# Layer 1 of a two-layer trunk: split input weights stored to DRAM in the first half of the tokens and loaded in the second

## The chip, the cores and the metric

One core of one Trainium2 chip runs the whole program. The time is the device time of one execution in microseconds; the median of three runs is compared.

## The reference, cut to what matters

The trunk has two layers over 2048 tokens of 1024 features, each `x = x + rms_norm(layer(rms_norm(x)))`. Layer 0 is attention beside a gated MLP. Layer 1, where the change lies, is a convolution module:

```python
def conv_layer(h, w_in, dw_w, dw_b, ln_g, ln_b, w_out):
    a, gl, z = jnp.split(h @ w_in, 3, axis=-1)
    y = a * jax.nn.sigmoid(gl)
    y = lax.conv_general_dilated(y, dw_w[:, None, :], window_strides=(1,),
                                 padding=((CONV_KERNEL - 1, 0),),
                                 dimension_numbers=('NWC', 'WIO', 'NWC'),
                                 feature_group_count=CONV_WIDTH) + dw_b
    y = jax.nn.silu(layer_norm(y, ln_g, ln_b))
    return (y * jax.nn.silu(z)) @ w_out
```

`w_in` is 1024 x 3072 and the depthwise convolution has 31 taps per channel. All data is float32.

## The kernel before

**Split products.** Float32 products are made of three matmuls on two rounded parts: an operand is cast to a high part (`hi`) and the remainder is kept as a low part (`lo`), and `hi*hi + hi*lo + lo*hi` is accumulated (`dense_T`, L152 to L165). The method `split` (L119 to L125) makes the parts: a cast on ACT (L122), then a subtraction (L125), on POOL for the weights of this layer.

**Layer 1, input.** `layer1_in` (L957) is run for tokens 0 to 1023 and again for tokens 1024 to 2047 (its argument `half`). Each half goes through the same 12 blocks of 256 weight columns, in slightly different orders (`GATED`, L45): eight of kind "g" (128 columns of `a` and 128 of the gate) and four of kind "z" (256 columns of `z`). So there are 24 blocks, numbered 0 to 23 here and `i` in the code. A block is four groups of 24 matmuls of 128x512; each group is a step of the generator, and a call of `beat` stands behind it. The inner function `load` (L963) fetches a block's weights into `wraw` (one buffer, 1 MB; L972, DMAs at L976) and splits them into `whiA`/`wloA` or `whiB`/`wloB`, in turn (L978 to L981). `weights` (L985) calls it one block ahead: the load of block i+1 is written at the start of block i, when the matmuls of block i-1, which used the same pair of tiles, have been issued.

**The convolution.** Each "g" block gives one `y` tile (128 channels, 1024 tokens), which joins a queue; its 31 taps are shared out between DVE and POOL. DVE does a tap in one instruction (`acc`, L1134). POOL needs a product by ACT (`prod`, L1100) and adds it (`cacc`, L1101). A finished channel block goes to `yc_d` in DRAM (L1143).

**The planner.** Who does which tap is settled while the program is written: `self.clock` has a booked time for DVE ("v") and POOL ("p"), `beat` (L1158) moves the planner's time by 5.12 us and gives out taps until both clocks have caught up, first to POOL and then to DVE. A tap books 1.2 us on DVE (L1136) or 2.4 us on POOL (L1102). Other work of these engines books time as well, so that fewer taps fall to them: a weight split books 4.5 us on POOL (L982).

**The tail.** `tail` (L1270) writes the steps in order: first half, the second half's normalised input (`load_hs`), second half with the first three chunks of `gated_norm` between its steps, then eight chunks of 256 tokens of output projection (`out2`), with the layer norm of the chunk two further on (`gated_norm`, L1175) between them. The norm of chunk 4 and later needs every channel of the convolution of the second half (`drain`, L1148 and L1186). The output weights are split by DVE (L1324).

**Order.** Each engine runs its queue in order. The build sorts the instructions into the queues by its own estimate of when each can start, with the written order as a guide, so neighbours in a queue are not always neighbours in the code. All DMAs of this layer are issued by SP, in the order of its queue: one that waits holds those behind it.

Of the kernel before, what the change touches and what calls it, by code (L numbers as in the profile page):

```python
# [10 lines left out]
F32 = mybir.dt.float32  # L11
F32R = mybir.dt.float32r
# [7 lines left out]
P = 128  # L20
S = 2048
D = 1024
KT = D // P
# [58 lines left out]
class Trunk:  # L82
# [151 lines left out]
    def setup(self):  # L234
        nc = self.nc
        self.odd = self.pool(self.ctx, "odd")
        edge = [self.pool(self.ctx, f"edge{side}", side=side) for side in (None, "right")]
        edge[0].tile([P, LEFT // 4], F32, name="left", tag="left")
        edge[1].tile([P, RIGHT // 4], F32, name="right", tag="right")
        c = self.c = self.pool(self.ctx, "const")  # L240
        dr = self.dr = self.pool(self.ctx, "spill", 1, DRAM)
        self.q_d = dr.tile([2, 512, S], F32, name="q_d", tag="q_d")
        self.ksw_d = dr.tile([2, 256, S], F32, name="ksw_d", tag="ksw_d")
        self.vsw_d = dr.tile([S, 4, P], F32, name="vsw_d", tag="vsw_d")
        self.kvc_d = dr.tile([256, S], F32, name="kvc_d", tag="kvc_d")
        self.a_d = dr.tile([D, S], F32, name="a_d", tag="a_d")
        self.bz_d = dr.tile([D, S], F32, name="bz_d", tag="bz_d")
        self.x1_d = dr.tile([S, D], F32, name="x1_d", tag="x1_d")
        self.yc_d = dr.tile([D, S], F32, name="yc_d", tag="yc_d")
        self.z_d = dr.tile([D, S], F32, name="z_d", tag="z_d")  # L250
        self.taps = self.tile(c, [P, KT, TAPS], F32, "taps")
        self.cb = self.tile(c, [P, KT], F32, "cb")
        self.ident = self.tile(c, [P, P], F32, "ident")
        make_identity(nc, self.ident)
        self.gpre = self.tile(c, [P, 2, KT], F32, "gpre")
# [701 lines left out]
    def layer1_in(self, inner, half, hs):  # L957

        nc, a, pool, conv = self.nc, self.a, self.lp, self.cp
        W = a["odd_w_in"][0]  # L960
        t0 = half * HALF

        def load():  # L963
            i = len(self.ws)
            if i == 24:
                return
            kind, k = self.plan[i]
            if kind == "g":
                pieces = [W[:, n * D + P * k:n * D + P * k + P] for n in range(2)]
            else:  # L970
                pieces = [W[:, 2 * D + 256 * k:2 * D + 256 * k + 256]]
            raw = self.tile(pool, [P, KT, 256], F32, "wraw")  # L972
            o = 0
            for p in pieces:
                w = p.shape[1]
                nc.sync.dma_start(raw[:, :, o:o + w], p.rearrange("(k p) n -> p k n", p=P))  # L976
                o += w
            where, tag = ((pool, "A"), (inner, "B"))[i % 2]  # L978
            hi = self.tile(where, [P, KT, 256], F32R, "whi" + tag)
            lo = self.tile(where, [P, KT, 256], F32R, "wlo" + tag)  # L980
            self.split(hi, lo, raw, nc.scalar, nc.gpsimd)  # L981
            self.busy("p", 4.5)  # L982
            self.ws.append((hi, lo))

        def weights():  # L985
            i = self.nw
            self.nw += 1
            while len(self.ws) < min(24, i + 2):
                load()
            return self.ws[i]  # L990

        def gated(k):
            w = weights()
            y = self.tile(conv, [P, HALF + 32], F32, "y", 6)
            if half:
                nc.scalar.copy(y[:, 0:32], self.hist[:, k])
            else:
                nc.gpsimd.memset(y[:, 0:32], 0.0)
            th = self.tile(pool, [P, 2, 512], F32, "b4", 5)
            for c in range(2):  # L1000
                o, = self.dense_T(w, P, hs[c:c + 1])
                nc.scalar.activation(th[:, c], o, AF.Tanh, scale=0.5)
                self.beat()
                yield
            for c in range(2):
                o, = self.dense_T(w, 0, hs[c:c + 1])
                nc.vector.scalar_tensor_tensor(y[:, 32 + 512 * c:544 + 512 * c], th[:, c], 1.0, o,  # L1007
                                               ALU.add, ALU.mult)
                self.busy("v", 0.6)
                if c == 0:  # L1010
                    self.beat()
                    yield
            if not half:
                nc.scalar.copy(self.hist[:, k], y[:, HALF:])
            self.queue.append(dict(k=k, half=half, y=y, tap=0, end=TAPS, acc=None, sum=None, bias=self.cb[:, k:k + 1]))
            self.beat()
            yield

        def zgate(k):
            w = weights()  # L1020
            st = [self.tile(pool, [P, 2, 512], F32, "b4", 5) for _ in range(2)]
            for c in range(2):
                for j in range(2):
                    o, = self.dense_T(w, P * j, hs[c:c + 1])
                    nc.scalar.activation(st[j][:, c], o, AF.Silu)  # L1025
                    self.beat()
                    yield
            for j in range(2):
                r = 256 * k + P * j
                nc.sync.dma_start(self.z_d[r:r + P, t0:t0 + HALF], st[j].rearrange("p c t -> p (c t)"))  # L1030

        for kind, k in self.plan[12 * half:12 * half + 12]:
            yield from (gated if kind == "g" else zgate)(k)
# [377 lines left out]
```

## Time and profile before

| what | value |
|---|---|
| runs | 2277.89, 2279.05 and 2279.7 us; median 2279.05 us |
| the profiled execution's own time | 2275.86 us |
| its span, first to last instruction | 2274.1 us |
| mean granted TensorE clock | 0.992 |
| busy, share of the span | PE 97%, DVE 68%, POOL 62%, ACT 55% |
| the first half's blocks begin at | 1520 us |
| the second half's block 14 begins at | 1839.7 us |
| output projection of layer 1 begins at | 2068.1 us |

Times within the execution are microseconds from the first instruction. A line such as L1134 is a line of the kernel. In a row of a group, "x304 | 378.9, 1281 | 4.0" means 304 instructions, 378.9 us busy in all, 1281 ns each in the mean, and 4.0 us in which the engine stood idle just before them. In a timeline row the first number is the start, the second the duration, and a bracket at the end gives the idle time before it and what ended it. PEclk is the granted TensorE clock as a share of full speed; the two levels are 2.4 GHz (1.00) and 1.2 GHz (0.50).

### The profile page before, as it was taken

Reading aid. Unit: us, or ns where it says so; the run is one execution under the profiler, and the core shown is the slowest. Engines: PE = TensorE matmul, PEld = TensorE weight load, DVE = VectorE, ACT = ScalarE, POOL = GpSimd, SP = SyncE. Lnnn points to the kernel's source line nnn. Section 1 sums busy time; section 2 is a strip of 40 time slices with the busy share of each in tenths; the row PEclk is TensorE's granted clock in tenths of the full one; section 3 lists DMA queues with packets and bytes.
Section 4 is the critical chain, followed back from the end, with each engine's and each line's share of the span. In section 5 each row is a group of like instructions: output and inputs, shape, how many; then the busy total and the mean of one; then the engine's idle time right before and its main releaser. Section 6 shows DMA issues by size and latency. Waiting matters only on the chain.

```text
span 2274.1 us, 34588 instructions
## 1 busy us (share of the span) xinstructions
PE 2202.5 (97%) x12414; PEld 1907.0 (84%) x12414; DVE 1547.0 (68%) x3272; ACT 1258.6 (55%) x2345; POOL 1400.6 (62%) x1351
## 2 busy tenths in 40 slices
PE   8999999999989999999999989999999989998998
PEld 7898889988878999898998978888888778886877
DVE  3441324365248998888889844527998899999772
ACT  5231232253258888878898854425555575556463
POOL 5232222243237778667789644548999579999683
PEclk9999999999999999999999999999999999999999
DMA  6252231442281111100113154651222432224641
GB/s 161 94 190 88 79 107 53 145 138 86 89 235 53 32 41 29 29 22 25 29 54 110 45 169 151 215 187 47 84 75 83 139 111 65 74 93 145 226 167 65
DMA packets 244860, 229.19 MB, mean 101 GB/s; under 512 B 33841, under 2 KB 206897, under 8 KB 244432
## 3 DMA queue, kind: packets, MB, share of 16 engines
q1 hardware_dynamic: 244688, 226.98, 31.5%
q8 instruction: 98, 1.61, 0.3%
q14 instruction: 74, 0.61, 0.1%
HBM read 157.73 MB, written 69.21 MB: 100 GB/s over the span
## 4 chain that ended last, share of the span: by engine, by line
PE 64%; DVE 15%; POOL 10%; issue 5%; ACT 3%; DMA 2%; SPq 1%; DVEq 0%; POOLq 0%; ACTq 0%
POOL cacc L1101 7%; PE T L708 7%; PE A L161 7%; PE A L162 7%; PE A L163 7%; DVE acc L1134 6%; PE O L731 4%; PE A L576 4%; PE O L730 4%; PE A L577 4%; PE A L844 4%; PE A L843 4%; PE A L842 4%; PE A L173 2%; PE A L175 2%
## 5 line engine op out<-in xcount | busy, mean ns | idle before, releaser
L1134 DVE SCALAR_TENSOR_TENSOR acc<-y,const_taps,acc 128x1024 f32<-128x1024 f32 x304 | 378.9, 1281 | 4.0
L1101 POOL TENSOR_TENSOR cacc<-cacc,prod 128x1024 f32<-128x1024 f32 x145 | 371.7, 2569 | 14.5 <-ACT prod L1100 7.2
L125 POOL TENSOR_TENSOR wlo<-wraw,whi 128x2048 fp32r<-128x2048 f32 (+1 forms) x26 | 120.8, 4647 | 314.8 <-ACT whi L122 279.5
L125 DVE TENSOR_TENSOR ptl<-T,pth 128x512 fp32r<-128x512 f32 (+1 forms) x414 | 263.8, 659 | 20.8 <-ACT pth L122 17.9
L122 ACT CAST pth<-T 128x512 fp32r<-128x512 f32 (+1 forms) x414 | 221.6, 579 | 50.4 <-PE T L708 40.3
L1100 ACT ACTIVATE prod<-y,const_taps 128x1024 f32<-128x1024 f32 x145 | 165.2, 1149 | 139.1 <-POOL cacc L1101 138.9
L161 PE MATMUL A<-hhi,whi 128*128 128x512 f32 x608 | 237.8, 391 | 0.0
L163 PE MATMUL A<-hhi,wlo 128*128 128x512 f32 x608 | 236.8, 389 | 0.0
L162 PE MATMUL A<-hlo,whi 128*128 128x512 f32 x608 | 236.8, 389 | 0.0
L685 POOL TENSOR_SCALAR Ps<-Ps,attn_ssm,gates 128x256 f32<-128x256 f32 (+15 forms) x128 | 161.1, 1259 | 110.9 <-DVE attn_ssm L682 77.9
L730 PE MATMUL O<-pth,V 128*128 128x256 f32 x824 | 220.7, 292 | 0.0
L731 PE MATMUL O<-ptl,V 128*128 128x256 f32 x824 | 219.5, 293 | 1.0 <-POOL ptl L717 0.4
L576 PE MATMUL A<-K,q 128*128 128x320 f32 (+4 forms) x544 | 206.7, 384 | 9.0 <-DVE attn_smx L580 4.4
L577 PE MATMUL A<-K,q 128*128 128x320 f32 (+4 forms) x544 | 183.7, 343 | 0.0
L680 ACT ACTIVATE Ps<-Ps,attn_nm 128x256 f32<-128x256 f32 (+15 forms) x128 | 155.8, 1217 | 31.3 <-DVE attn_nm L678 29.2
L580 DVE CUSTOM_DVE_ANT_1 Ps<-A,attn_bm 128x512 f32<-128x512 f32 (+3 forms) x264 | 154.8, 611 | 22.9 <-PE A L577 11.4
L708 PE MATMUL T<-ident,Ps 128*128 128x128 f32 x1088 | 164.3, 273 | 2.2 <-DVE ptl L125 1.8
L731 PEld LDWEIGHTS O<-ptl,V 128*128 128x128 f32 x824 | 155.6, 189 | 8.5 <-DVE ptl L125 4.2
L730 PEld LDWEIGHTS O<-pth,V 128*128 128x128 f32 x824 | 155.7, 189 | 2.5
L162 PE MATMUL A<-h,whiA 128*128 128x512 f32 x384 | 151.1, 394 | 0.0
L161 PE MATMUL A<-h,whiA 128*128 128x512 f32 x384 | 150.3, 393 | 0.7 <-DVE y L1007 0.7
L161 PE MATMUL A<-h,whiB 128*128 128x512 f32 x384 | 149.7, 390 | 1.2 <-ACT b L1025 1.2
(388 smaller groups left out, 6197.1 us busy)
## 6 DMA issues: line engine op xcount, KB each, us to landing
wraw<-in_even_w_in_dram SPq DMA_DIRECT2D x24, 1024.0 KB, 6.0
q<-q_d SPq DMA_DIRECT2D x128, 128.0 KB, 2.8
wraw<-in_odd_w_in_dram SPq DMA_DIRECT2D x32, 512.0 KB, 4.6
x<-x_d SPq DMA_DIRECT2D x21, 512.0 KB, 3.3
a_d<-osum SPq DMA_DIRECT2D x128, 64.0 KB, 2.1
x<-in_x_dram SPq DMA_DIRECT2D x16, 512.0 KB, 5.6
x_d<-x SPq DMA_DIRECT2D x16, 512.0 KB, 2.6
wraw<-in_odd_w_in_dram SPq DMA_DIRECT2D x8, 1024.0 KB, 4.9
```

Of the source, the lines that this page charges most:

```text
L122: self.nc.scalar.copy(hi, src)
L125: lo_eng.tensor_tensor(lo, src, hi.bitcast(F32), ALU.subtract)
L161: nc.tensor.matmul(o, whi[:, k, wk], hhi[:, k], start=(k == 0), stop=False)
L162: nc.tensor.matmul(o, whi[:, k, wk], hlo[:, k], start=False, stop=False)
L163: nc.tensor.matmul(o, wlo[:, k, wk], hhi[:, k], start=False, stop=(k == KT - 1))
L576: nc.tensor.matmul(out, q[:, 0, r, :], K[:, g, ks], start=True, stop=False)
L577: nc.tensor.matmul(out, q[:, 1, r, :], K[:, g, ks], start=False, stop=True)
L708: nc.tensor.transpose(pt[:, c:c + P], ps[r], self.ident)
L730: nc.tensor.matmul(O, v, hi[:, c], start=(i + j == 0), stop=False)
L731: nc.tensor.matmul(O, v, lo[:, c], start=False, stop=(i + j == len(items) - 1))
L1101: nc.gpsimd.tensor_tensor(c["sum"], c["sum"], t, ALU.add)
L1134: v.scalar_tensor_tensor(acc, win, w, old, ALU.mult, ALU.add)
```

## The change

Blocks 0 to 11 split their weights as before, and each then writes the two parts to a DRAM tile of its kind and number, `w_d`, with two DMAs of 1 MB. Blocks 12 to 23 issue two DMAs of 1 MB that load the ready parts straight into the `whi` and `wlo` tiles; they load no `wraw`, make no cast and no subtraction, and book nothing on POOL's clock.

```diff
+        self.w_d = dr.tile([12, 2, P, KT * 256], F32, name="w_d", tag="w_d")
...
             kind, k = self.plan[i]
+            where, tag = ((pool, "A"), (inner, "B"))[i % 2]
+            hi = self.tile(where, [P, KT, 256], F32R, "whi" + tag)
+            lo = self.tile(where, [P, KT, 256], F32R, "wlo" + tag)
+            flat = lambda t: t.rearrange("p k n -> p (k n)").bitcast(F32)
+            kept = self.w_d[k + 8 * (kind == "z")]
+            if i >= 12:
+                for t, d in zip((hi, lo), kept):
+                    nc.sync.dma_start(flat(t), d)
+                self.ws.append((hi, lo))
+                return
             if kind == "g":
...
-            where, tag = ((pool, "A"), (inner, "B"))[i % 2]
-            hi = self.tile(where, [P, KT, 256], F32R, "whi" + tag)
-            lo = self.tile(where, [P, KT, 256], F32R, "wlo" + tag)
             self.split(hi, lo, raw, nc.scalar, nc.gpsimd)
+            for t, d in zip((hi, lo), kept):
+                nc.sync.dma_start(d, flat(t))
             self.busy("p", 4.5)
             self.ws.append((hi, lo))
```

## Rows read from the trace of the kernel before

**Rows 1.** The profile's page: busy time and share of each engine.

```profile
PE 2202.5 (97%) x12414; PEld 1907.0 (84%) x12414; DVE 1547.0 (68%) x3272; ACT 1258.6 (55%) x2345; POOL 1400.6 (62%) x1351
```

**Rows 2.** Busy time by stretch; after the engines granted clock, DMA share, GB/s.

```profile
1500.00:1760.00 260.00, 260.00 (x1148) 215.06 (x1147) 211.11 (x172) 136.33 (x149) 227.59 (x103) 1.00 0.26 87
1760.00:1880.00 120.00, 109.14 (x494) 88.14 (x493) 110.17 (x90) 71.12 (x89) 83.33 (x29) 0.97 0.36 119
1880.00:2060.00 180.00, 180.00 (x796) 149.06 (x795) 178.98 (x143) 102.58 (x105) 175.28 (x64) 1.00 0.23 80
2060.00:2110.00 50.00, 41.40 (x164) 32.91 (x163) 46.74 (x40) 28.61 (x35) 49.02 (x18) 0.90 0.52 178
2110.00:2200.00 90.00, 84.50 (x364) 68.87 (x363) 76.89 (x70) 48.35 (x86) 64.72 (x25) 0.98 0.55 196
```

**Rows 3.** Timeline of PE, 2060 to 2110 us: all three matmuls that waited.

```profile
2073.48 0.50 PE L843 MATMUL A<-h,h 128*128 128x512 f32 x1 [2.26 <-DVE h L125]
...
2085.22 0.50 PE L843 MATMUL A<-wloB,h 128*128 128x512 f32 x1 [1.43 <-DVE wloB L125]
...
2100.86 0.77 PE L842 MATMUL A<-whiA,h 128*128 128x512 f32 x1 [4.92 <-DVE yn L874]
```

**Rows 4.** Timelines of DVE and POOL in the same stretch.

```profile
2073.35 9.62 DVE L1134 SCALAR_TENSOR_TENSOR acc<-y,const_taps,acc 128x1024 f32<-128x1024 f32 x8
...
2083.42 15.04 POOL L1101 TENSOR_TENSOR cacc<-cacc,prod 128x1024 f32<-128x1024 f32 x4 [0.43 <-ACT prod L1100]
```

**Rows 5.** Groups by line and shape, 1500 to 2110 us.

```profile
L1134 DVE SCALAR_TENSOR_TENSOR acc<-y,const_taps,acc 128x1024 f32<-128x1024 f32 x304 | 378.9, 1281 | 4.0
...
L1101 POOL TENSOR_TENSOR cacc<-cacc,prod 128x1024 f32<-128x1024 f32 x145 | 371.7, 2569 | 14.5 <-ACT prod L1100 7.2
L125 POOL TENSOR_TENSOR wloA<-wraw,whiA 128x2048 fp32r<-128x2048 f32 x12 | 56.5, 4706 | 20.0 <-ACT whiA L122 19.9
L125 POOL TENSOR_TENSOR wloB<-wraw,whiB 128x2048 fp32r<-128x2048 f32 x12 | 56.0, 4664 | 4.6 <-ACT whiB L122 2.8 <-PE T L212 1.8
...
L1100 ACT ACTIVATE prod<-y,const_taps 128x1024 f32<-128x1024 f32 x145 | 165.2, 1149 | 139.1 <-POOL cacc L1101 138.9
L122 ACT CAST whiB<-wraw 128x2048 fp32r<-128x2048 f32 x13 | 24.8, 1907 | 8.1 <-PE A L162 7.6 <-DMA wraw<-in_odd_w_out_dram 0.5
```

**Rows 6.** Timelines of PE and POOL: blocks 22 and 23 begin; block 23's low part.

```profile
2024.59 0.39 PE L161 MATMUL A<-h,whiA 128*128 128x512 f32 x1
...
2046.35 0.39 PE L161 MATMUL A<-h,whiB 128*128 128x512 f32 x1
...
2033.39 4.61 POOL L125 TENSOR_TENSOR wloB<-wraw,whiB 128x2048 fp32r<-128x2048 f32 x1
```

**Rows 7.** Waits of SP's queue, 1500 to 2274 us: total, times, longest.

```profile
SPq L976 <- POOL wloB L125: 113.0, 10, 18.8
...
SPq L976 <- POOL wloA L125: 111.0, 12, 17.9
```

**Rows 8.** DMA issues, 1500 to 2110 us; then GB/s in 40 slices of 1760 to 1880 us.

```profile
wraw<-in_odd_w_in_dram SPq DMA_DIRECT2D x8, 1024.0 KB, 4.9
z_d<-b SPq DMA_DIRECT2D x16, 512.0 KB, 2.6
...
GB/s 0 175 8 175 0 124 374 26 175 0 8 167 125 366 210 241 338 124 0 29 288 340 372 159 215 0 0 0 0 175 175 5 0 115 235 3 0 0 0 0
```

**Rows 9.** Timeline of SP: a store of the convolution behind block 22's start.

```profile
2035.65 0.32 SPq L1143 DMA_DIRECT2D yc_d<-cout  x1
```

**Rows 10.** Timelines of DVE, POOL and PE, 1824 to 1865 us; last, L1214's group.

```profile
1824.77 5.58 DVE L1214 TENSOR_TENSOR y<-x,Y 128x1024 f32<-128x1024 f32 x1
...
1824.64 4.62 POOL L125 TENSOR_TENSOR wloA<-wraw,whiA 128x2048 fp32r<-128x2048 f32 x1 [4.54 <-ACT whiA L122]
...
1864.87 0.77 PE L1207 MATMUL T<-y,mean 128*128 128x256 f32 x1 [4.32 <-DVE y L1203]
...
L1214 DVE TENSOR_TENSOR y<-x,x 128x1024 f32<-128x1024 f32 x2 | 2.4, 1222 | 3.1 <-DMA x<-yc_d 3.1
```

## The prediction, made before the changed kernel was run

> **What bounds the kernel now.** I read the page's busy times first: PE is busy for 97% of the span, all others far less [rows 1]. A share of the whole span hides stages, so the table by stretch comes next [rows 2]. From 1500 to 1760 us and from 1880 to 2060 us PE is busy without a break at a granted clock of 1.00: there the projection's matmuls are the time, and nothing that is taken from another engine can shorten them. What can be won lies where PE stands idle: 120 - 109.14 = 10.86 us between the halves, 50 - 41.40 = 8.60 us at the start of the output projection (2060 to 2110), 5.50 us behind it. In the second stretch the clock is also 0.90 of full, that is at 1.2 GHz for part of it, after each of three idle times; 0.10 x 50 = 5.0 us are lost by that.
>
> The second thing to see in that table is what DVE and POOL do: from 1880 to 2060 they are busy for 178.98 and 175.28 of 180 us. Both run the taps of the convolution at their limit beside a PE that is at its own, and they fall behind it. The timeline of PE shows the bill: the three waits from 2060 to 2110 are ended by DVE, twice by a split of output weights and once by the work on an output tile [rows 3]. The timelines of DVE and POOL show what stands in the queue around those: runs of taps, eight in a row on DVE at 2073 and four on POOL from 2083 [rows 4]. So the unfinished convolution sets the loss in this stretch, and PE's own work sets the rest.
>
> **What the change removes.** In the second half 12 casts on ACT and 12 subtractions on POOL: 12 x 1.91 = 22.9 us of ACT and 12 x 4.69 us (the mean of 4.706 and 4.664) = 56.2 us of POOL [rows 5]. Alone that would buy nothing where PE is the limit. But the planner's bookings go too: 12 x 4.5 = 54 us of POOL's clock are free, and the planner fills them with taps. If n taps pass from DVE to POOL and both then end T sooner, 2.4 n = 54 - T and 1.2 n = T, so n = 15 and T = 18. Going through the bookings beat by beat, with whole taps and the sums that join the two engines' parts, I get 14 more sums on POOL and 13 fewer instructions on DVE, and the last tap given out three beats (15.4 us) sooner. In measured durations [rows 5]: DVE is 13 x 1.281 = 16.7 us ahead at the end of the convolution; POOL 56.2 - 14 x 2.569 = 20.2 us; ACT 22.9 - 14 x 1.149 = 6.8 us.
>
> **What that is worth.** Each wait from 2060 to 2110 is at most 4.92 us [rows 3], less than either lead, and the work that delayed it is what got shorter. So I count all 8.60 us of idle time and, with them, the 5.0 us of low clock: 13.6 us. The waits after 2110 (5.50 us) I leave as they are: there DVE works on the norms, with 76.89 of 90 us busy and no convolution [rows 2]. The 10.86 us between the halves I leave too; bounds of 0 and 14.5 us (10.86 and 0.03 x 120 = 3.6 of clock) go into the range.
>
> **What it adds in the first half.** 24 stores of 1 MB. No row has a store of 1 MB. One of 0.5 MB landed after 2.6 us, and neighbouring transfers reached 374 GB/s in a slice [rows 8]. Two stores (2.10 MB) thus take between 5.6 us (2.10 / 0.374) and 10.4 us (4 x 2.6). I take 6.8: 2.6 for the first half megabyte and 1.57 / 0.374 = 4.2 for the rest, as DMAs that are issued together overlapped in the rows. On SP the stores wait for the end of the subtraction. The next `wraw` load waits for the same event already (113.0 and 111.0 us of waits in all) [rows 7], so the stores' wait holds nothing that was free to go. But the load now lands behind the stores. That makes a ring: stores 6.8, load 4.9 [rows 8], cast 1.9, one tap ahead on POOL 2.6, subtraction 4.7, in all 20.9 us. A block takes 2046.35 - 2024.59 = 21.76 us, and the low part was ready at 2038.00, 8.35 us before its use [rows 6]. The ring is shorter than a block, so I cost it at nothing; matmuls of the block before cover it. With the upper end of 10.4 us it is 24.5 us, longer than a block, and the cover would be used up. That is the slower rival below.
>
> **What it adds in the second half.** Two loads of 1 MB a block, in place of one. They can start only when the block before last has released its tiles, since the prefetch into `wraw` one block earlier is gone. One load landed after 4.9 us [rows 8]; two take between 5.6 us and 9.8 us, and I take 4.9 + 1.05 / 0.374 = 7.7. Of a block's 21.76 us some 14 are spare, against 8.35 before. The new wait on PE is SP's; behind it in the queue stand stores of `z_d` and `yc_d` and loads for the norms. These hold the weights as well where they come first. The store of a finished channel block left at 2035.65, 11.06 us after block 22 had begun [rows 9], because DVE was late with it. Weights queued behind it would land at 2035.97 + 7.7 = 2043.7, still 2.7 us before 2046.35; with 9.8 us, 0.6 us before. With DVE 16.7 us further on such a store leaves sooner. I cost this at nothing, with little to spare. Instruction counts, the DRAM tile and the moved lines that allocate tiles cost nothing in a stretch that PE fills.
>
> **The sum** is made on the profiled execution: 2275.86 - 13.6 = 2262.3 us (its span of 2274.1 lies 1.8 below its own time). That execution is 3.2 us below the median of 2279.05, so for the median the same saving gives 2279.05 - 13.6 = 2265.4 us.
>
> **Rival 1: more is won, between the halves too** (2251 to 2259). At 1824.77 DVE began a sum (L1214) that took 5.58 us; the same instruction took 1.22 us elsewhere. POOL's subtraction ran from 1824.64 for 4.62 us, and the chain behind the sum made PE wait 4.32 us at 1864.87 [rows 10]. The subtraction goes. If half of the 14.5 us goes with it, the time is 2265.4 - 7.2 = 2258.2; if all, 2250.9. Against it: POOL fills the place with norm sums and taps of 2.57 us [rows 5], and DVE meets those instead.
>
> The Trainium skill (SBUF — State Buffer, section "Who interferes with whom") says that a DVE instruction with two SBUF inputs and a GpSimd instruction that reads SBUF exclude each other for a whole instruction. The row above agrees: 5.58 us is about the 4.62 us of the subtraction and 1.22 us of work less the 0.13 us between their starts, 5.71 us. By that rule shorter POOL instructions shorten the longest wait, but 14 more of them leave many chances for a short one.
>
> **Rival 2: the saving meets the next wait** (about 2275). The longest of the three waits, 4.92 us, ended with the work on an output tile, which needs results of PE and ACT besides DVE's turn. If only the two weight splits come sooner, 2.26 + 1.43 = 3.7 us are saved: 2275.4. For it: DVE and PE take turns in the tail, so a lead on one does not last. Against it: taps lie between the pieces of that work.
>
> **Rival 3: slower, by the ring of stores in the first half** (about 2287). With the upper end it takes 24.5 us against 21.76, 2.7 us lost a block and 30 us over 11 blocks. The lead of 8.35 us takes some of it; 21.8 us stall PE, and 13.6 come off again: 2279.05 + 8.2 = 2287.3. It decides once the ring is over 22.5 us (21.76 + 8.35 / 11). For it: the first half has its own `yc_d` and `z_d` stores, which the ring leaves out. Against it: the overlap in rows 8, and a DMA share of 0.26 in that stretch [rows 2]. Late weights in the second half would show in the same way, but PE's wait there also lets DVE catch up.
>
> **Chances.** The forecast 0.50, rival 1 0.20, rival 2 0.15, rival 3 (with late weights) 0.15. A measurement of this kernel can tell about 0.2% (4.6 us) from no change. Forecast and rival 1 are faster by more than that, 0.70; rival 2 is within it, 0.15; rival 3 is slower, 0.15. The range reaches from rival 1 in full (2251) to a little above no change (2281), which leaves out rival 3 alone; the forecast's own range is 2259 to 2271.
>
> **What would show it.** Right: L1101 at about 159 instructions and the taps of L1134 some 16 fewer; POOL's subtractions of `wraw` halved to 12; DVE and POOL still full from 1880 to 2060, but the last `yc_d` store 15 to 20 us sooner against the start of the output projection; PE without waits on DVE in the first 50 us of it, at a clock near 1.00; PE as full as before in both halves. Wrong: a wait of PE's first matmul of a block on a weight DMA; in the first half a subtraction that ends later from block to block; PE's waits at the start of the output projection as long as before, though DVE's taps are gone. If PE idles less there and more after 2110, rival 2 holds.

## The result, and the profile after

The changed kernel takes 2295.28 us (median of six runs, 2293.73 to 2301.75). The kernel before takes 2279.38 us in the same comparison, and the ratio is 1.0079 (95% interval 1.0069 to 1.0090). It is slower by 0.8%; the forecast of 2265.4 us and its range to 2281 both missed it. The profiled execution's span is 2292.0 us, 17.9 us more than before.

The first view is busy time by stretch, for the changed kernel. The columns are those of [rows 2]: PE, PEld, DVE, ACT, POOL, then granted clock, DMA share and GB/s.

```profile
1500.00:1760.00 260.00, 260.00 (x1148) 215.06 (x1147) 210.89 (x172) 136.22 (x149) 227.60 (x103) 1.00 0.53 180
1760.00:1880.00 120.00, 111.59 (x500) 90.78 (x499) 103.07 (x91) 68.73 (x90) 74.35 (x29) 0.94 0.48 171
1880.00:2060.00 180.00, 180.00 (x796) 149.03 (x795) 155.09 (x125) 92.97 (x101) 143.30 (x57) 1.00 0.32 120
2060.00:2110.00 50.00, 44.27 (x186) 35.73 (x185) 44.38 (x35) 30.47 (x39) 44.92 (x17) 0.97 0.50 168
2110.00:2200.00 90.00, 67.26 (x274) 53.68 (x273) 70.75 (x66) 42.15 (x69) 67.33 (x27) 0.89 0.45 158
```

Read PE's column first. Up to 2110 us PE is not worse off than in [rows 2]: full in both projections, 2.45 us less idle between the halves (at a clock of 0.94 instead of 0.97), 2.87 us less from 2060 to 2110. The loss is in the last row: 22.74 us idle instead of 5.50, at a clock of 0.89 instead of 0.98. Its cause stands in the third row, where PE shows nothing: DVE is busy for 155.09 us instead of 178.98, POOL for 143.30 instead of 175.28. Some 24 and 32 us of the convolution's two engines go unused, in a stretch in which they were at their limit. In the kernel before, POOL did 54 sums and 8 weight subtractions (38 us) there; without the subtractions it does 55 sums, so the time that was freed bought one sum.

The groups by line and shape, 1510 to 2270 us, of the changed kernel (L1144 is L1134 of before, L1111 is L1101):

```profile
L1144 DVE SCALAR_TENSOR_TENSOR acc<-y,const_taps,acc 128x1024 f32<-128x1024 f32 x291 | 362.9, 1281 | 3.8
...
L1111 POOL TENSOR_TENSOR cacc<-cacc,prod 128x1024 f32<-128x1024 f32 x159 | 398.1, 2509 | 57.1 <-ACT cacc L1106 29.7 <-ACT prod L1110 14.3 <-ACT cacc L1104 5.2
...
L125 POOL TENSOR_TENSOR wloB<-wraw,whiB 128x2048 fp32r<-128x2048 f32 x6 | 28.2, 4703 | 2.8 <-ACT whiB L122 2.8
```

The counts are those predicted: 14 more sums on POOL, 13 fewer convolution instructions on DVE, half of the subtractions gone. (L1144 in all its forms is at 308, 16 fewer than before; the row shows its commonest form, 304 before. Two more sums join the engines' parts.) New is the right end of the second row: POOL stood idle for 57.1 us ahead of its sums (14.5 in [rows 5]), and 29.7 of them wait for ACT's L1106. That instruction starts a new channel's sum in a `cacc` tile. There are two such tiles.

The timelines of POOL, ACT, DVE and PE follow this wait to the end:

```profile
2025.90 17.30 POOL L1111 TENSOR_TENSOR cacc<-cacc,prod 128x1024 f32<-128x1024 f32 x7 [24.93 <-ACT cacc L1106]
...
2024.58 1.24 ACT L1106 ACTIVATE cacc<-y,const_cb,const_taps 128x1024 f32<-128x1024 f32 x1 [11.39 <-DVE cout L1150]
...
2049.26 1.89 ACT L122 CAST whiA<-wraw 128x2048 fp32r<-128x2048 f32 x1
...
2051.18 4.11 DVE L125 TENSOR_TENSOR wloA<-wraw,whiA 128x2048 fp32r<-128x2048 f32 x1 [19.21 <-ACT whiA L122]
...
2146.43 1.23 DVE L1150 TENSOR_TENSOR cout<-acc,cacc 128x1024 f32<-128x1024 f32 x1 [5.87 <-POOL cacc L1111]
...
2147.71 0.80 PE L843 MATMUL A<-whiB,h 128*128 128x512 f32 x1 [15.88 <-DVE cout L1150]
```

POOL has run ahead with two channels' sums; for a third, ACT waits until DVE has finished a channel (L1150) and so freed a tile. POOL is idle for 24.93 us. Then DVE runs into the split of the first output weights: its high part goes into `whiA`, which PE reads until block 22 ends. Block 22 ends at 2045.04, ACT's queue reaches the cast at 2049.26, and DVE, which does its queue in order, stands for 19.21 us with taps behind it. In the kernel before, DVE was so late with its taps that it met this split at 2054.49 without a wait. The time that both lost comes back as taps in the output projection, and the last channel is summed at 2146.43, 40 us later than before (2106.82). PE needs it: at chunk 2 the accumulators' PSUM pool is closed and its banks go to the output tiles, so the matmul at 2147.71 waited for that sum.

The four longest of PE's waits from 2060 to 2200 us, by total (us, times, longest), show that this is the loss:

```profile
PE A L843 <- DVE cout L1150: 15.9, 1, 15.9
PE A L843 <- DVE yn L875: 5.0, 1, 5.0
PE A L844 <- DVE wloB L125: 3.0, 1, 3.0
PE A L843 <- ACT prod L1110: 2.7, 1, 2.7
```

The transfers were as forecast, or better. DMA issues of the changed kernel, first 1500 to 1760, then 1830 to 2050 us (count, KB each, median us to landing):

```profile
w_d<-wloA SPq DMA_DIRECT2D x6, 1024.0 KB, 5.2
w_d<-whiB SPq DMA_DIRECT2D x6, 1024.0 KB, 3.8
...
wraw<-in_odd_w_in_dram SPq DMA_DIRECT2D x4, 1024.0 KB, 7.7
...
wloB<-w_d SPq DMA_DIRECT2D x5, 1024.0 KB, 6.9
...
wloA<-w_d SPq DMA_DIRECT2D x4, 1024.0 KB, 7.7
```

A pair of loads took 6.9 to 7.7 us against the estimate of 7.7; the pair of stores 5.2 against 6.8. The `wraw` load took 7.7 where the forecast's ring had 4.9. No matmul of a block waits for any of them.

### The profile page after: what moved, and what is told of

The parts are those of the page before. It is cut to its first block, busy times and chain, and to the rows that moved or that the text cites. A ratio compares the mean times of both kernels' runs of the same rounds, so it can differ in the third digit from the quotient of the medians.

```text
span 2292.0 us, 34646 instructions
## 1 busy us (share of the span) xinstructions
PE 2205.1 (96%) x12414; PEld 1908.4 (83%) x12414; DVE 1529.4 (67%) x3259; ACT 1255.5 (55%) x2348; POOL 1377.6 (60%) x1353
## 4 chain that ended last, share of the span: by engine, by line
PE 61%; DVE 15%; POOL 12%; issue 5%; ACT 3%; DMA 2%; SPq 1%; DVEq 0%; POOLq 0%; ACTq 0%
POOL cacc L1111 9%; PE T L709 7%; PE A L161 7%; PE A L162 7%; PE A L163 7%; DVE acc L1144 7%; PE O L732 4%; PE A L577 4%; PE O L731 4%; PE A L578 4%; PE A L845 3%; PE A L844 3%; PE A L843 3%; PE A L177 2%; PE A L173 2%
## 5 line engine op out<-in xcount | busy, mean ns | idle before, releaser
L1111 POOL TENSOR_TENSOR cacc<-cacc,prod 128x1024 f32<-128x1024 f32 x159 | 398.1, 2509 | 57.1 <-ACT cacc L1106 29.7
L1144 DVE SCALAR_TENSOR_TENSOR acc<-y,const_taps,acc 128x1024 f32<-128x1024 f32 x291 | 362.9, 1281 | 3.8
L125 DVE TENSOR_TENSOR ptl<-T,pth 128x512 fp32r<-128x512 f32 (+1 forms) x414 | 263.7, 659 | 20.6 <-ACT pth L122 17.8
L1110 ACT ACTIVATE prod<-y,const_taps 128x1024 f32<-128x1024 f32 x159 | 181.5, 1149 | 138.5 <-POOL cacc L1111 138.3
L161 PE MATMUL A<-h,whiB 128*128 128x512 f32 x384 | 150.9, 393 | 1.0 <-ACT b L1035 1.0
L162 PE MATMUL A<-h,whiA 128*128 128x512 f32 x384 | 150.5, 392 | 0.0
L162 PE MATMUL A<-h,whiB 128*128 128x512 f32 x384 | 150.5, 392 | 0.0
```

The source lines that it names most:

```text
L125: lo_eng.tensor_tensor(lo, src, hi.bitcast(F32), ALU.subtract)
L161: nc.tensor.matmul(o, whi[:, k, wk], hhi[:, k], start=(k == 0), stop=False)
L162: nc.tensor.matmul(o, whi[:, k, wk], hlo[:, k], start=False, stop=False)
L1111: nc.gpsimd.tensor_tensor(c["sum"], c["sum"], t, ALU.add)
L1144: v.scalar_tensor_tensor(acc, win, w, old, ALU.mult, ALU.add)
```

## The experiments

Theory A, after this reading: the planner, freed of its bookings, gives POOL sums for which there is no tile, both engines wait, and the backlog lands on the output projection. Theory B, the rival: the transfers hold the queue or the memory. Times are compared with runs of the kernel before on the same chip: 2276.02 us for the first four kernels, 2276.96 for the next four, 2277.58 for the last three.

**Bookings kept** (the changed kernel, but the planner still books the subtraction that is gone).

```diff
             if i >= 12:
...
+                self.busy("p", 4.5)
                 self.ws.append((hi, lo))
```

> Two theories of the 16 us that the changed kernel is slower. Theory A: the planner's bookings are at fault. With 54 us of POOL's clock unbooked it hands out taps in an order that the two engines can't follow: POOL stands idle 24.9 us for an accumulator that DVE still holds, DVE 19.2 us before the split of the first output weights, and the last channel's sum ends 40 us later. Theory B: the transfers are at fault (24 stores and 24 loads of 1 MB on SP's queue and the DMA engines). This run keeps stores and loads and gives the second half's 12 bookings of 4.5 us back, so the taps are shared out as before the change (145 sums on POOL, 304 taps in DVE's main group). A: 2265 to 2282 us, the last yc_d store near 2110 us again or sooner, no wait of PE over 6 us after 2060. B: 2290 us or more, as the changed kernel.

Measured 2273.04 us, ratio 0.9982 (0.9972 to 0.9991). The time booked for nothing is worth 22 us against the changed kernel: POOL now has 31 us idle from 1880 to 2060 and DVE none to speak of. First its row of busy time, then its waits of PE from 2060 to 2110.

```profile
1880.00:2060.00 180.00, 180.00 (x796) 149.09 (x795) 178.24 (x151) 97.07 (x105) 149.09 (x60) 1.00 0.32 122
...
PE A L843 <- DVE yn L875: 6.6, 1, 6.6
```

Theory A's time holds, and so does the last store (2102.55); its limit of 6 us for PE's waits was missed. All that was taken from POOL and ACT buys 3 us: DVE keeps its 304 taps, and PE's longest wait is still the one behind an output tile (6.6 us; 4.92 in [rows 3]).

**Stores alone** (the kernel before, and the 24 stores of the first half; the second half splits as before).

```diff
             self.split(hi, lo, raw, nc.scalar, nc.gpsimd)
+            if i < 12:
+                for t, d in zip((hi, lo), kept):
+                    nc.sync.dma_start(d, flat(t))
```

> The kernel before with the 24 stores of the first half added and nothing else: the second half splits its weights and books them as before. A: within 0.2% of before, 2275 to 2284 us. B, if the stores are the part of the traffic that hurts: 2285 us or more, with waits of PE in the first half or in the step between the halves.

Measured 2276.36 us, ratio 1.0001 (0.9992 to 1.0010). In the first half PE is full beside a DMA share that has doubled:

```profile
1500.00:1760.00 260.00, 260.00 (x1148) 215.12 (x1147) 211.56 (x172) 136.16 (x149) 227.60 (x103) 1.00 0.53 180
```

The stores cost nothing. Theory B falls for them.

**Plan alone** (the kernel before without the bookings of blocks 12 to 23; it still splits all weights, and stores none).

```diff
-            self.busy("p", 4.5)
+            if i < 12:
+                self.busy("p", 4.5)
```

> The kernel before, without any of the new transfers, with the second half's 12 bookings taken away: POOL splits the weights as before and gets the 14 more sums besides. A: slower than before, 2285 to 2310 us, since POOL is 36 us longer (14 x 2.57) at work and the last channel's sum is late. B: without transfers nothing of the loss is there, so about 2279 us.

Measured 2327.16 us, ratio 1.0220 (1.0205 to 1.0235), without any transfer of the change. By stretch from 1880 to 2060, and PE's waits from 2060 to 2250:

```profile
1880.00:2060.00 180.00, 179.38 (x791) 148.19 (x790) 152.36 (x117) 94.50 (x97) 162.41 (x60) 1.00 0.22 76
...
PE A L842 <- DVE cout L1141: 37.9, 2, 25.4
```

Theory B falls, and the loss is above the 2310 us that theory A allowed. PE waits for the same join of the last sums as in the changed kernel, and longer. So the moved taps make a loss without any transfer. It is not the changed kernel's loss alone: POOL still has the subtractions to do, and its own wait for a tile, on L1097, is only 8.2 us from 1880 to 2060. How much each of the two adds was not taken apart.

**A third tile** (the changed kernel, three tiles for POOL's sums).

```diff
-            c["sum"] = self.tile(self.cp, [P, HALF], F32, "cacc", 2)
+            c["sum"] = self.tile(self.cp, [P, HALF], F32, "cacc", 3)
```

> The changed kernel with three accumulators for POOL's sums (cacc) in place of two. A: POOL's wait of 24.9 us for an accumulator goes or shrinks below 8 us, the last yc_d store comes 15 us or more sooner than in the changed kernel, and the time is 2270 to 2288 us. B: 2290 us or more, as the changed kernel.

Measured 2274.36 us, ratio 0.9989 (0.9979 to 0.9999). POOL's group from 1880 to 2060, then PE's waits from 2060 to 2110:

```profile
L1111 POOL TENSOR_TENSOR cacc<-cacc,prod 128x1024 f32<-128x1024 f32 x67 | 168.2, 2517 | 10.0 <-ACT prod L1110 6.0
...
PE A L844 <- DVE wloB L125: 3.1, 1, 3.1
PE A L845 <- POOL h L125: 1.5, 2, 1.4
```

With the same counts (159 and 291) 67 sums are done in this stretch; the changed kernel did 55. Its wait of 24.9 us is gone, and so is DVE's of 19.21 and PE's of 15.88. Theory A holds. But the kernel stands at 2274, not at the forecast.

**The split on POOL** (the changed kernel, the first output-weight subtraction moved from DVE to POOL).

```diff
-            wout = lambda which, w=None: self.wout_pieces(..., which, w, self.nc.vector)
+            wout = lambda which, w=None: self.wout_pieces(..., which, w, self.nc.gpsimd if which == [0] else self.nc.vector)
```

> The changed kernel, but the first output-weight split (of the four pieces) has its subtraction on POOL, so that DVE does not wait 19.2 us for the weight tile that block 22 still uses. Theory A (planner and the two tiles of POOL sums): POOL now stands in that wait instead, behind it its taps, and DVE's sums wait for POOL; the order of the queues is otherwise that of the changed kernel, so PE's wait on the last channel's sum stays at some 10 to 20 us and the time at 2285 to 2300. Theory D (DVE's wait for the weight tile alone is the cause): DVE ends its taps some 15 us sooner, PE's wait on the channel's sum goes, and the time comes to 2270 to 2280.

Measured 2301.0 us, ratio 1.0104 (1.0088 to 1.0121). Theory D falls. Theory A has the direction, but the time is 1 us above its range, and PE's wait on the last channel's sum shrank to 1.5 us; PE waits instead behind an output tile (11.2 us, L875) and the layer norm (7.5 us, L1213). The timelines of POOL and DVE show where the wait went:

```profile
2021.13 27.21 POOL L1111 TENSOR_TENSOR cacc<-cacc,prod 128x1024 f32<-128x1024 f32 x11 [24.93 <-ACT cacc L1106]
2048.30 4.63 POOL L125 TENSOR_TENSOR wloA<-wraw,whiA 128x2048 fp32r<-128x2048 f32 x1
...
2055.32 3.41 DVE L1144 SCALAR_TENSOR_TENSOR acc<-y,const_taps,cacc 128x1024 f32<-128x1024 f32 x1 [28.12 <-POOL cacc L1111]
```

DVE no longer waits for `whiA`, but for POOL's sum of the next channel, and longer: 28.12 us. So DVE's 19.21 us were not the first cause; POOL's lost 24.93 us stand before either.

**Three tiles without the change**, with all bookings, and with half of them (the kernel before; the changed kernel with 4.5 and with 2.25 us booked a block).

```diff
-            c["sum"] = self.tile(self.cp, [P, HALF], F32, "cacc", 2)
+            c["sum"] = self.tile(self.cp, [P, HALF], F32, "cacc", 3)
...
             if i >= 12:
...
+                self.busy("p", 4.5)
```

The first kernel has the edit of the tiles only, the second both, the third both with 2.25 in the place of 4.5.

> The kernel before with a third tile for the POOL sums and nothing else. Theory A (the two tiles bound POOL only once the bookings are gone): POOL's sums waited little in the kernel before, so the time is 2273 to 2279, within 0.2% of it. Rival E (the third tile is a gain by itself, and the change then adds nothing to it): 2265 to 2274, no slower than the changed kernel with three tiles.

> The changed kernel with the bookings kept and three tiles. Theory A: tap counts as in the kernel before (304 and 145), POOL freed of 56 us of subtractions, nothing waits for a tile: 2269 to 2275, that is as the kernel with bookings alone or a few us less. If the freed POOL time only pays when taps are moved to it, this stays at 2273.

> The changed kernel with half of the booking (2.25 us a block) and three tiles, so some 7 taps move to POOL. Theory A: DVE and POOL both get a lead that neither loses in a wait for a tile: 2266 to 2273, below both the kernel with full bookings and the one with none. Rival (the tail's own order of norms and splits bounds it, whatever the lead): 2273 to 2275, the same as those.

Measured 2275.19 us (0.9991, 0.9982 to 1.0001), 2273.68 (0.9988, 0.9978 to 0.9999) and 2275.67 (0.9990, 0.9980 to 0.9999). The third tile is no gain by itself, but the rest of rival E holds: the changed kernel with three tiles (0.9989) is not measurably faster than the kernel before with three (0.9991), so with the loss mended the change is worth nothing that these runs can tell. The second kernel fits both of its theories. For half of the bookings theory A's 2266 to 2273 missed and its rival was nearer: a lead shared by both engines is worth no more than one that POOL has alone. All these kernels, like the ones with bookings or with a third tile, lie within 0.2% of the kernel before.

**A planner that counts the tiles** (the changed kernel with its two tiles; `sums` rises when a sum is begun and falls when DVE takes it over).

```diff
+        free = self.sums < 2
-        q = [c for c in self.queue if room(c, 1)]
+        q = [c for c in self.queue if room(c, 1) and (c["sum"] or free)]
...
-            q = [c for c in self.now if room(c, 1 if c["sum"] else 6)]
+            q = [c for c in self.now if room(c, 1 if c["sum"] else 6) and (c["sum"] or free)]
```

> The changed kernel with two tiles of POOL sums as it has them, and a planner that counts them: it starts no third sum before DVE's instructions have taken one over. The counts stay at 160 and 290. Theory A (what costs the 16 us is that the planner gave POOL sums for which there was no tile): POOL's wait of 24.9 us on ACT goes to less than 10, the wait on the last channel's sum goes, and the time comes to 2272 to 2280. Rival (the two tiles are too few for so many sums, however they are given out): 2285 or more, with POOL waiting as before.

Measured 2275.89 us, ratio 0.9989 (0.9978 to 1.0001). POOL's group from 1880 to 2060 in this kernel (L1113 is L1111):

```profile
L1113 POOL TENSOR_TENSOR cacc<-cacc,prod 128x1024 f32<-128x1024 f32 x67 | 166.4, 2488 | 13.3 <-ACT prod L1112 5.9 <-ACT cacc L1106 3.0 <-ACT cacc L1108 0.5
```

No tile is added and no tap taken back (160 sums on POOL, one more than in the changed kernel), and the loss is gone: 67 sums instead of 55 in the stretch. So two tiles are enough; what cost 16 us was a plan that did not know of them.

**Less convolution** (the changed kernel with three tiles, and a shorter convolution in the second half). The question left is why no version reaches 2265.

```diff
-            self.queue.append(dict(k=k, half=half, y=y, tap=0, end=TAPS, acc=None, ...))
+            self.queue.append(dict(k=k, half=half, y=y, tap=0, end=15 if half else TAPS, acc=None, ...))
```

> The changed kernel with three tiles, and the second half's convolution cut from 31 taps per channel to 15: it leaves out 16 of the 31. That is the most that any lead of DVE and POOL can give: some 50 us less work on DVE and 100 on POOL. Theory of the forecast (PE's waits from 2060 to 2110 are the backlog of taps, and go with it): 2274.4 - 6.7 of waits - 1.5 of clock = 2266 or less, PE at 49 of 50 us or more in that stretch. Rival T (the waits belong to the output projection's own chains: weights reloaded into one raw tile, cast, subtracted, and the norm behind each output tile): 2270 to 2274, and PE still waits 5 us or more there.

Measured 2265.28 us, ratio 0.9948 (0.9932 to 0.9965). By stretch, and PE's only wait from 2060 to 2110:

```profile
2060.00:2110.00 50.00, 49.09 (x217) 40.30 (x216) 23.42 (x25) 19.13 (x29) 19.63 (x8) 1.00 0.59 203
...
PE A L844 <- DVE wloB L125: 0.9, 1, 0.9
```

The forecast's theory holds and rival T falls: without a backlog the waits are gone, the clock is 1.00, and the time is near the one forecast (12 us are saved against the same chip's 2277.58, where the forecast had 13.6). But this kernel leaves out far more work than the change could: it is the bound of what a lead can give.

**Another raw tile** (the changed kernel with three tiles; third and fourth piece of the output weights exchange their raw tiles).

```diff
-            ... [(lp, "wraw")] * 3 + [(lp, "h6")] ...
+            ... [(lp, "wraw")] * 2 + [(lp, "h6"), (lp, "wraw")] ...
```

> The changed kernel with three tiles; the third piece of the output weights is loaded into the tile that the fourth used, and the fourth into the raw tile, so the third's load need not wait for the second's subtraction. Rival T: PE's wait on the subtraction of the third piece (3.1 us) shrinks to below 1, the time by 2 to 4 us to 2270 to 2273. Theory of the forecast (taps on DVE set that wait): no change, 2274.

Measured 2278.7 us, ratio 1.0005 (0.9996 to 1.0014), a miss for both. The wait grew: PE stood 3.7 us for the third piece's high part and 2.8 us more before the matmul that first uses its low part. The timeline of SP says why:

```profile
2073.06 0.38 SPq L816 DMA_DIRECT2D wraw<-in_odd_w_out_dram  x1
2075.28 0.32 SPq L849 DMA_DIRECT2D x<-x_d  x1
...
2076.17 0.38 SPq L816 DMA_DIRECT2D h<-in_odd_w_out_dram  x1
```

The load into `h6`, now the third piece, left last in SP's order, at 2076.17; in the kernel with three tiles the same piece's load left at 2070.26. Of these 5.9 us 2.8 are no delay: that execution was 2.8 us later already (the second piece's load left at 2061.34 against 2058.55). The other 3.1 us are the place in the queue: the two loads leave where they left before, `wraw` first and `h6` behind a load of `x`, and only the pieces in them are exchanged. The piece that is needed first now stands last.

## Why the prediction was wrong

**The step that failed** is "What the change removes", where it turns the planner's arithmetic into leads: "DVE is 13 x 1.281 = 16.7 us ahead at the end of the convolution; POOL 56.2 - 14 x 2.569 = 20.2 us". The counts and the durations were right, but a lead was computed as work left out, as if both engines would stay full. I went through the bookings beat by beat and not through the tiles that the given-out work needs. The view that could have warned was at hand. These are ACT's groups that begin a sum in a `cacc` tile, in the kernel before, 1500 to 2110 us:

```profile
L1096 ACT ACTIVATE cacc<-y,const_cb,const_taps 128x1024 f32<-128x1024 f32 x16 | 19.9, 1242 | 13.3 <-DVE acc L1134 6.3 <-DVE y L1007 5.2 <-DVE cout L1140 1.8
...
L1094 ACT ACTIVATE cacc<-y,const_taps 128x1024 f32<-128x1024 f32 x10 | 11.5, 1152 | 12.4 <-DVE acc L1134 11.7 <-DVE cout L1140 0.8
```

ACT already stood 20.6 us there for DVE's L1134 and L1140, where DVE takes a sum over and so frees its tile; in the kernel before with a third tile and nothing else, 4.4 us are left of that. So the two tiles already held ACT up, and POOL hardly felt it (14.5 us idle in [rows 5]). A plan that gives POOL more sums without counting tiles could run into this, and did. The convolution ended 40 us later, not 16.7 earlier. Kept bookings, a third tile or a planner that counts to two each take this loss away (2273.0, 2274.4, 2275.9 us); the bookings' removal alone, without any transfer, makes a larger one (2327.2 us). So it is shown that sums given out without a tile make this loss. Why the build put the split of the first output weights where DVE met it too early was not tried apart from POOL's wait; with a third tile and with the counting planner, DVE meets the same split without a wait.

**The term that was too large** is the 13.6 us itself. "Each wait is at most 4.92 us, less than either lead": this measured a backlog by the waits it causes. The taps left after 2060 us measure it (groups of DVE and POOL from 2060 to 2150: first the kernel before, then the changed one, then the one with three tiles).

```profile
L1134 DVE SCALAR_TENSOR_TENSOR acc<-y,const_taps,acc 128x1024 f32<-128x1024 f32 x23 | 28.6, 1279 | 0.1
...
L1101 POOL TENSOR_TENSOR cacc<-cacc,prod 128x1024 f32<-128x1024 f32 x11 | 35.6, 3236 | 1.1 <-ACT prod L1100 0.4
```

```profile
L1144 DVE SCALAR_TENSOR_TENSOR acc<-y,const_taps,acc 128x1024 f32<-128x1024 f32 x28 | 35.9, 1283 | 0.6
...
L1111 POOL TENSOR_TENSOR cacc<-cacc,prod 128x1024 f32<-128x1024 f32 x18 | 45.1, 2510 | 7.8 <-ACT cacc L1106 4.8 <-ACT cacc L1104 2.6
```

```profile
L1144 DVE SCALAR_TENSOR_TENSOR acc<-y,const_taps,acc 128x1024 f32<-128x1024 f32 x14 | 18.0, 1286 | 0.4
...
L1111 POOL TENSOR_TENSOR cacc<-cacc,prod 128x1024 f32<-128x1024 f32 x7 | 18.9, 2694 | 0.5
```

Before, 28.6 us of taps on DVE and 35.6 us of sums on POOL lie in the output projection. A lead of 16.7 and 20.2 us is a little over half of that. With three tiles 14 and 7 are left, so the leads that came out are 10.6 and 16.7 us, and PE still stands idle for 50 - 43.28 = 6.72 us from 2060 to 2110 (clock 0.97). These are not the same waits grown shorter: the one behind the output tile fell from 4.92 to 0.73 us, the one for the low part `wloB` grew from 1.43 to 3.12, and waits on ACT (1.4) and POOL (1.5) are new. With no taps left PE stands idle for 0.91, and nearly the forecast's time comes out. That the taps hold PE there was right; the size of the backlog was not looked at. The 13.6 us also count about 1.2 us twice: the clock is low (0.50) from 2075 to 2078 and from 2099 to 2105 us, after two of the three waits and not after the one of 1.43, and from 2098 to 2100.86 us PE stands idle at a granted clock of 0.59 (0.41 x 2.86 = 1.2 us), a time that is in the 8.60 us already.

**What was right.** The stores, costed at nothing: shown by the kernel that has only them. The second half's loads, costed at nothing: the bookings kernel has them and loses nothing in the projection. The planner's counts. And that PE, full in both projections, gains nothing there.

**The rivals.** Rival 1 did not come: the subtraction beside L1214 is gone, and PE idles 2.45 us less between the halves, but the clock is lower there (0.94). Rival 2 named the time that every mended version reaches (2273 to 2276). Its reason, that the wait behind an output tile stays, fits the kernel with bookings (6.6 us); with three tiles that wait is nearly gone and others stay, so there the time came out by luck. Rival 3 had the sign and a time of 2287, but its mechanism, the ring of stores, is excluded. The case that decided, two engines that run out of tiles when more is given to one of them, was among none of them; "DVE and POOL still full from 1880 to 2060" was the check that named it, and the first row that failed.

## What to carry to other kernels

Time that is freed on an engine is a gain only if the work moved into it finds its buffers free: before counting a planner's extra work as a lead, walk the tiles that it needs, and who releases them, in the order of each engine's queue. Measure a backlog by the instructions that are left behind the deadline, not by the waits that they cause: half a backlog removed left most of the waits here. And when a booking stands for work that is taken out, take the booking out as a change of its own: it moved 22 us here, the work itself 3 to 4.

## What the runs showed of the hardware

PE held 260.00 us of 260 at a clock of 1.00 while the share of the DMA engines rose from 0.26 to 0.53, so 180 GB/s of transfers, the stores among them, cost the matmuls beside them nothing measurable (87 GB/s before). The same subtraction on DVE, 128x2048 from two SBUF tiles, took between 2.28 and 4.48 us in these runs. The timelines of DVE in the kernel with three tiles and in the one with fewer taps show both:

```profile
2080.31 4.06 DVE L125 TENSOR_TENSOR wloB<-wraw,whiB 128x2048 fp32r<-128x2048 f32 x1 [0.93 <-ACT whiB L122]
```

```profile
2076.02 2.29 DVE L125 TENSOR_TENSOR wloB<-wraw,whiB 128x2048 fp32r<-128x2048 f32 x1 [1.49 <-ACT whiB L122]
```

In the first, POOL ran four sums from 2072.41 to 2082.22; in the second POOL stood idle until 2077.58. The last of those sums ended 1.91 us after the subtraction had begun; 1.91 + 2.29 = 4.20 us is near the 4.06. The Trainium skill (SBUF — State Buffer, section "Who interferes with whom") says that the two engines exclude each other for a whole instruction where both use their shared port; these two rows agree with it, and no run here was made for it alone. A convolution tap on DVE whose accumulator lies in PSUM, the memory that PE writes, so that only `y` is a large SBUF input, stayed at 1.28 us (1279 to 1286 ns in the groups above). The tap that takes POOL's sum over has a second large SBUF input, `cacc`. In the changed kernel it took 1.29 us while POOL stood idle:

```profile
1993.53 1.29 DVE L1144 SCALAR_TENSOR_TENSOR acc<-y,const_taps,cacc 128x1024 f32<-128x1024 f32 x1 [0.59 <-POOL cacc L1111]
```

The same instruction took 3.41 us at 2055.32 in the kernel with the split on POOL (its row is above), where POOL had begun a subtraction at 2055.25.
